# Holding retention's outgoing states, and its first incoming ones, behind gate, f and q evacuations in a hybrid decoder step

## The chip, the core and the metric

The kernel runs on one core of a Trainium2 chip. The metric is the device time of one execution in microseconds (us); the kernel before takes 2566.82 us, the median of three runs (2566.23 to 2566.89).

## The reference, cut to what matters

One decoder layer: a half-step feed-forward network, a mixer, a second half-step feed-forward network, each with a residual and a layer norm. There are 280 tokens: 16 meta tokens, 256 prompt tokens and 8 sample tokens with recurrent states of their own. All matrices are float32.

```python
q_r, k_r, v_r, g_r, q_h, f_h, i_h, g_h, a_r, a_h = jnp.split(x @ w_in, N_PROJ, axis=-1)
...
# retention, per head: the state that comes in is decayed, gets k v added, and goes out
S_new = jnp.exp(lg * C)[:, None, None].astype(S.dtype) * S + jnp.einsum('bhjd,bhjv->bhdv', k_dec, v)
...
y = jax.nn.sigmoid(a_r) * o_r + jax.nn.sigmoid(a_h) * o_h
return y @ w_out, s_ret, s_hg
```

Retention has 8 heads. For each head the 8 sample tokens bring a state of 256 x 256 numbers in and take one out: 2 MB in and 2 MB out for each head, which the kernel moves in four pieces of 512 KB. HGRN2, the other half of the mixer, has 16 heads with smaller states.

## The kernel before, in words

**Weights.** Every matrix is read once from memory in pieces of 512 KB, each with eight blocks of 128 x 128. `stream` issues such a piece as one DMA on SyncE's queue (SP) into a tile `raw` (three buffers); ScalarE (ACT) makes of it a rounded copy `whi` (L188) and VectorE (DVE) the rest `wlo` (L189); both have three buffers. For each block TensorE (PE) does three matmuls (L218): `xh,whi`, `xl,whi`, `xh,wlo`. So a piece feeds 24 matmuls. A piece can be loaded only when the piece three earlier has been split, and split only when PE is done with the piece three earlier.

**The mixer stage.** The projection `w_in` is computed in eight units, one for each retention head, counted from 0. `project` runs six groups for unit u, in the order `f`, `q_h`, `i_h`, `q_r`, `k_r`, `v_r`, and then four groups of gates of unit u-1 (`g_r` with `a_r`, `g_h` with `a_h`, twice). A group is four pieces of weights (96 matmuls), a steady unit 40 pieces. When a group is done, `evacuate` takes its sums out of PSUM: for the gates a sigmoid on ACT of each half (L690, L693, tiles `gs`) and products on DVE; for `f` a sigmoid (L653) and a scaling (L654) on ACT for each of two columns of chunks; for `q_h` a sigmoid (L660) and a product on DVE.

**Mixing in the gaps.** `mix_hg` and `mix_ret` are generators. `pump` advances them after each step of a projection, and a `yield n` lets n steps go by; so their work lies between the projection's matmuls. The order on PE is the program's. On ACT, DVE, GpSimd (POOL) and SP a scheduler sets the order from the program's, from priorities and from its own estimate of when operands are ready. A weights' DMA has high priority.

**Retention's states.** `mix_ret(u)` starts three steps after `v_r` of unit u was evacuated, that is under the gates of unit u-1. It takes tiles of one tag, `smr`, with four buffers: `ks` and `vs` (split keys and values), then two for the states' first half (`load(0)`), and when `ks` and `vs` are used up two for the second half (`load(1)`). ACT decays each piece (L1192), by a factor `gam` that POOL makes; DVE adds keys times values (L1198); then the two pieces of a half are stored to `srs` (L1202). Later PE multiplies the states with the queries (`pqr`, L1211). The buffers come free when the store has landed and `pqr` is done. In the kernel before, the states go out as soon as each half is computed, and the next unit's first half is loaded as soon as its buffers are free.

**SP's queue.** All of these loads and stores are issued by SP, one after another: a DMA whose operands aren't ready holds up all that stand behind it, weights among them.

Of the kernel before, what the change touches and what calls it, by code (L numbers as in the profile page):

```python
# [14 lines left out]
ALU = mybir.AluOpType  # L15
# [3 lines left out]
P = 128  # L19
# [9 lines left out]
HR, HG = 8, 16  # L29
# [99 lines left out]
def trunk(ctx: ExitStack, tc: tile.TileContext, A, O):  # L129
# [109 lines left out]
    def mul(out, a, b):  # L239
        nc.vector.tensor_tensor(out=out, in0=a, in1=b, op=ALU.mult)  # L240
# [306 lines left out]
    with tc.tile_pool(name="yp", bufs=1) as yp:  # L547
# [7 lines left out]
        with tc.tile_pool(name="mp", bufs=1) as mp:  # L555
# [7 lines left out]
            def tmp(name, shape=(P, T), bufs=1, dt=F32, tag=None):  # L563
                if name in rows:
                    rows[name] = rows[name][1:] + rows[name][:1]
                    return rp.tile(list(shape), dt, tag=rows[name][-1], name=name)
                return mp.tile(list(shape), dt, tag=tag or name, name=name, bufs=bufs)
# [80 lines left out]
            def evacuate(n, c0, c1, o0, o1, b0, b1):  # L648
                if n == "f":
                    f = tmp("f", (P, 2, T))  # L650
                    k = tmp("k", (P, 2, T))
                    for j, (c, o, b) in enumerate(((c0, o0, b0), (c1, o1, b1))):
                        nc.scalar.activation(f[:, j, :], o, AF.Sigmoid, **bias(b))  # L653
                        nc.scalar.activation(f[:, j, :], f[:, j, :], AF.Identity, scale=olb[:, c : c + 1], bias=lb[:, c : c + 1])  # L654
                    nc.scalar.activation(k, f, AF.Identity, scale=-1.0, bias=1.0)
                    st["f"], st["k"] = f, k
                elif n == "q_h":
                    q = tmp("q", (P, 2, TL))
                    for j, (o, b) in enumerate(((o0, b0), (o1, b1))):
                        nc.scalar.activation(q[:, j, :], o, AF.Sigmoid, **bias(b))  # L660
                        mul_biased(q[:, j, :], o, b, q[:, j, :])
                    st["q"] = q
                elif n == "i_h":
                    v = st.pop("i_h", None)
                    if v is None:
                        v = tmp("v", (P, 2, T))
                        nc.scalar.copy(v[:, 0, :], o0)
                        nc.scalar.copy(v[:, 1, :], o1)

                    start(mix_hg(c0 // 2, st["f"], st["k"], st["q"], v), {0: 20, 2: 46}.get(c0, 4))  # L670
                elif n in ("q_r", "k_r"):
                    sc, w, x0 = (1.0, TL, NMETA) if n == "q_r" else (KSC, T, 0)
                    r = tmp(n, (P, 2, w))
                    for j, (a, b, op) in enumerate(((cos, sin, ALU.subtract), (sin, cos, ALU.add))):
                        t = tmp("rot", (P, w), bufs=2)
                        for to, o, s, x in ((r[:, j, :], o0, b0, a), (t, o1, b1, b)):
                            nc.vector.scalar_tensor_tensor(
                                out=to, in0=o, scalar=sc if s is None else s, in1=x[:, x0:],
                                op0=ALU.mult if s is None else ALU.add, op1=ALU.mult)
                        nc.vector.tensor_tensor(out=r[:, j, :], in0=r[:, j, :], in1=t, op=op)  # L680
                    st[n] = r
                elif n == "v_r":
                    v = tmp("v", (P, 2, T))
                    nc.scalar.copy(v[:, 0, :], o0)
                    nc.scalar.copy(v[:, 1, :], o1)
                    start(mix_ret(c0 // 2, st["q_r"], st["k_r"], v), 24 if c0 == 2 else 3)
                elif n in ("g_r", "g_h"):
                    sg = tmp("gs", (P, TL), bufs=2)
                    t = tmp("gt", (P, TL), bufs=2)
                    nc.scalar.activation(sg, o0, AF.Sigmoid)  # L690
                    mul(t, sg, o0)
                    sa = tmp("gs", (P, TL), bufs=2)
                    nc.scalar.activation(sa, o1, AF.Sigmoid)  # L693
                    mul(t, t, sa)
                    u, e = divmod(c0, 2)
                    while u not in (done_r if n == "g_r" else done_h):
                        pump()
                    if n == "g_r":
                        y = tmp("y", (P, TL))
                        mul(y, t, on_r[u][:, e, :])  # L700
                        st["y"] = y
                    else:
                        y = st["y"]
                        nc.vector.scalar_tensor_tensor(
                            out=t, in0=t, scalar=ngt[:, c0 : c0 + 1], in1=on_h[u][:, e, :], op0=ALU.mult, op1=ALU.mult)

                        ys[c0] = y if c0 < EARLY else yp.tile([P, TL], F32, tag=f"y{c0}", name=f"y{c0}")
                        add(ys[c0], y, t)
                        if c0 < EARLY:
                            split(yh[c0], yl[c0], y)  # L710
# [374 lines left out]
            def mix_ret(u, q, k, v):  # L1085
                vt = tmp("vtr", (P, 2, 2, P))

                ks, vs = (tmp(n, (P, 2, 2, 2 * P), dt=F32R, bufs=4, tag="smr") for n in ("ks", "vs"))
                calm = 2
                sms = []  # L1090

                def load(e):
                    for c in range(2):
                        sms.append(tmp("smr", (P, 4, 256), bufs=4))
                        nc.sync.dma_start(sms[2 * e + c], A["sr"][u, c, :, 4 * e : 4 * e + 4, :])

                load(0)
# [91 lines left out]
                for e in range(2):  # L1189
                    ss = sms[2 * e : 2 * e + 2]  # L1190
                    for sm in ss:
                        nc.scalar.activation(sm, sm, AF.Copy, scale=gams[e])  # L1192
                    for i in (2 * e, 2 * e + 1):
                        for c in range(2):
                            for b in (2 * i, 2 * i + 1):
                                x, t = ss[c][:, b - 4 * e, :], LP + b
                                kk = late_k[:, c, b - 4 : b - 3] if e else k[:, c, t : t + 1]
                                nc.vector.scalar_tensor_tensor(  # L1198
                                    out=x, in0=vbs[i][:, b - 2 * i, :], scalar=kk, in1=x, op0=ALU.mult, op1=ALU.add)
                        spread(i + 2)  # L1200
                    for c in range(2):
                        nc.sync.dma_start(O["srs"][u, c, :, 4 * e : 4 * e + 4, :], ss[c])  # L1202
                    yield 1 if e else 10 if u == 0 else 6
                yield (11 if u == 0 else 15) + 2 * calm
                pq = mx_bank("pqr")
# [7 lines left out]
                                sms[2 * e + c][:, j, :], start=e + c == 0, stop=e + c == 2, tile_position=(0, 32 * j))  # L1213
                mul(scr2[:NB2], pq[:NB2, 256 : 256 + NMETA], dt[:NB2, c2:])
                upper_upper_lower(sc2, scr2[:NB2])
                os = tmp("osr", (P, 256))
                nc.scalar.copy(os, pq[:, :256])
                centre(os.unsqueeze(1))
# [158 lines left out]
```

## Time and profile before

| what | value |
|---|---|
| time, median of 3 runs | 2566.82 us (2566.23 to 2566.89) |
| span of the profiled execution, first to last instruction | 2563.9 us |
| around it, by the median of the runs | 2.9 us |
| granted TensorE clock | 1.000 |
| weights of `w_in` | 320 DMAs of 512 KB, median 4.3 us from issue to landing |
| retention's states in | 32 DMAs of 512 KB, median 5.0 us |
| retention's states out | 32 DMAs of 512 KB, median 6.7 us |

The profile is of one execution. Its span leaves out the start and the end of the program: against the median of the runs that is 2566.82 - 2563.9 = 2.9 us, and in this sense the profiled execution's own time is 2566.8 us. In rows of a timeline the first number is the start in us from the span's start, the second the duration in us. "POOL" is GpSimd, "SPq" the issue of a DMA by SyncE. In a row of a stage, the numbers behind the stretch are its length and then each engine's busy time with its count of instructions.

### The profile page before, as it was taken

To read this page: it belongs to the slowest core of one execution; us is meant where nothing else is said; L and a number is where in the kernel's file an instruction comes from. 1 tells how busy PE (TensorE), PEld (TensorE's weight loads), DVE (VectorE), ACT (ScalarE), POOL (GpSimd) and SP (SyncE) were. 2 spreads that over 40 slices of the span, in tenths; PEclk is the share of its full clock that TensorE was granted. 3 is DMA by queue.
4 is the path that set the end of the run, shared out by engine and by line. 5 is a ranking of instruction groups with operands and counts; after the bars stand their busy time and mean duration, and the time that the engine had idled before them with its cause. 6 is when DMAs were issued, how large, how long until landed. Compare 5 with 4: busy or idle time off the path is not lost.

```text
span 2563.9 us, 56275 instructions
## 1 busy us (share of the span) xinstructions
PE 2553.4 (100%) x23424; PEld 2534.4 (99%) x23424; DVE 1702.8 (66%) x2827; ACT 1392.2 (54%) x2186; POOL 57.0 (2%) x152
## 2 busy tenths in 40 slices
PE   9999999999999999999999999999999999999999
PEld 9999999999999999999999999999999999999998
DVE  6444544475569878777777777777885555556555
ACT  5444444444456767767676666675564444444443
POOL 0000000000000000000000000000000000000000
PEclk9999999999999999999999999999999999999999
DMA  7555555555555876767676767675556565565554
GB/s 244 183 187 183 187 182 184 186 182 186 184 201 180 287 265 232 264 214 260 212 264 215 259 223 255 224 239 188 196 190 197 194 197 195 194 196 195 195 195 149
DMA packets 156897, 536.26 MB, mean 209 GB/s; under 512 B 17952, under 2 KB 25952, under 8 KB 156640
## 3 DMA queue, kind: packets, MB, share of 16 engines
q1 hardware_dynamic: 156352, 532.37, 62.0%
q8 instruction: 183, 3.00, 0.5%
q14 instruction: 74, 0.61, 0.1%
q10 hardware_dynamic: 288, 0.29, 0.0%
HBM read 501.99 MB, written 30.61 MB: 208 GB/s over the span
## 4 chain that ended last, share of the span: by engine, by line
PE 96%; DVE 2%; ACT 0%; issue 0%; DMA 0%; SPq 0%; ACTq 0%; DVEq 0%
PE up L218 36%; PE dn L218 19%; PE pj_i_h L218 3%; PE pj_g_r L218 3%; PE pj_q_h L218 3%; PE pj_g_h L218 3%; PE pj_a_r L218 3%; PE pj_a_h L218 3%; PE pj_f L218 3%; PE pj_q_r L218 3%; PE pj_k_r L218 3%; PE wo L218 3%; PE pj_v_r L218 3%; DVE wlo L189 1%; PE pqr L1211 1%; PE psr L1168 0%
## 5 line engine op out<-in xcount | busy, mean ns | idle before, releaser
L189 DVE TENSOR_TENSOR wlo<-raw,whi 128x1024 fp32r<-128x1024 f32 (+1 forms) x869 | 1062.2, 1223 | 740.7 <-ACT whi L188 737.3
L188 ACT CAST whi<-raw 128x1024 fp32r<-128x1024 f32 (+1 forms) x870 | 905.7, 1042 | 909.2 <-PE up L218 411.0
L218 PE MATMUL up<-xh,whi 128*128 128x280 f32 (+1 forms) x2624 | 725.6, 280 | 0.6 <-ACT whi L188 0.6
L218 PE MATMUL up<-xh,wlo 128*128 128x280 f32 (+1 forms) x2624 | 725.8, 280 | 0.4 <-DVE wlo L189 0.3
L218 PE MATMUL up<-xl,whi 128*128 128x280 f32 (+1 forms) x2624 | 725.4, 279 | 0.0
L218 PEld LDWEIGHTS up<-xh,wlo 128*128 128x128 f32 x2624 | 492.6, 189 | 1.0 <-DVE wlo L189 1.0
L218 PEld LDWEIGHTS up<-xh,whi 128*128 128x128 f32 x2624 | 492.6, 189 | 0.8 <-ACT whi L188 0.8
L218 PEld LDWEIGHTS up<-xl,whi 128*128 128x128 f32 x2624 | 492.6, 189 | 0.0
L218 PE MATMUL dn<-hh,whi 128*128 128x280 f32 (+1 forms) x1376 | 384.7, 280 | 0.0
L218 PE MATMUL dn<-hh,wlo 128*128 128x280 f32 (+1 forms) x1376 | 384.3, 279 | 0.0
L218 PE MATMUL dn<-hl,whi 128*128 128x280 f32 (+1 forms) x1376 | 384.3, 279 | 0.0
L218 PEld LDWEIGHTS dn<-hh,whi 128*128 128x128 f32 x1376 | 260.1, 189 | 0.1
L218 PEld LDWEIGHTS dn<-hl,whi 128*128 128x128 f32 x1376 | 260.1, 189 | 0.1
L218 PEld LDWEIGHTS dn<-hh,wlo 128*128 128x128 f32 x1376 | 260.1, 189 | 0.0
L218 PE MATMUL pj_k_r<-xh,whi 128*128 128x280 f32 x256 | 74.2, 290 | 0.0
L218 PE MATMUL pj_g_r<-xh,whi 128*128 128x264 f32 x256 | 74.0, 289 | 0.0
L218 PE MATMUL pj_v_r<-xh,whi 128*128 128x280 f32 x256 | 73.8, 288 | 0.0
L218 PE MATMUL pj_v_r<-xh,wlo 128*128 128x280 f32 x256 | 72.4, 283 | 0.3 <-DVE wlo L189 0.3
L218 PE MATMUL pj_g_h<-xh,whi 128*128 128x264 f32 x256 | 72.7, 284 | 0.0
L218 PE MATMUL pj_k_r<-xh,wlo 128*128 128x280 f32 x256 | 72.4, 283 | 0.0
L218 PE MATMUL pj_v_r<-xl,whi 128*128 128x280 f32 x256 | 72.3, 283 | 0.0
L218 PE MATMUL pj_k_r<-xl,whi 128*128 128x280 f32 x256 | 72.3, 283 | 0.0
(421 smaller groups left out, 5263.4 us busy)
## 6 DMA issues: line engine op xcount, KB each, us to landing
raw<-in_w_up SPq DMA_DIRECT2D x343, 512.0 KB, 4.1
raw<-in_w_in SPq DMA_DIRECT2D x320, 512.0 KB, 4.3
raw<-in_w_dn SPq DMA_DIRECT2D x172, 512.0 KB, 3.5
smr<-in_sr SPq DMA_DIRECT2D x32, 512.0 KB, 5.0
out_srs<-smr SPq DMA_DIRECT2D x32, 512.0 KB, 6.7
raw<-in_w_out SPq DMA_DIRECT2D x32, 512.0 KB, 3.9
vbr<-vrd SPq DMA_DIRECT2D x32, 256.0 KB, 4.1
smh<-in_sg SPq DMA_DIRECT2D x16, 512.0 KB, 5.2
```

The lines of the kernel that those rows point to most:

```text
L188: nc.scalar.copy(hi[:, j:jn, :], raw[:, j:jn, :])
L189: nc.vector.tensor_tensor(out=lo[:, j0:j1, :], in0=raw[:, j0:j1, :], in1=hi[:, j0:j1, :].bitcast(F32), op=ALU.subtract)
L218: nc.tensor.matmul(o, w, t, start=start, stop=stop)
L1211: nc.tensor.matmul(pq[32 * j : 32 * j + 32, :256], qdr_at[c][:, 32 * b : 32 * b + 32], sms[2 * e + c][:, j, :], start=e + c == 0, stop=e + ...
```

## The change

It has three parts, all for units u > 1, that is for six of the eight:

- The stores of a unit's states aren't issued when the states are ready. A new generator, `outgoing`, is started where `pqr` is multiplied, 23 steps later it handles the first half and another 16 steps later the second. For each half POOL copies one column into a tile `zero`, clears it, and adds it to one column of each of the half's two pieces; then the pieces are stored. The column copied is the last gate's sigmoid (`st["seen"]`) for the first half and the next unit's `f` for the second (in the last unit, which has no next, the latest gate's sigmoid again). So a store waits, by way of POOL, for that evacuation. What is added is zero; the states stay the same.
- Before each of the two DMAs of `load(0)`, POOL copies one column of `st["q"]`, the HGRN2 queries of the unit itself, into the buffer, which makes the load wait for the evacuation of `q_h`.
- `evacuate` notes the gate's sigmoid in `st["seen"]`.

```diff
                     nc.scalar.activation(sa, o1, AF.Sigmoid)
+                    st["seen"] = sa
...
                 calm = 2
+                held = u > 1
                 sms = []
 
                 def load(e):
                     for c in range(2):
                         sms.append(tmp("smr", (P, 4, 256), bufs=4))
+                        if e == 0 and u > 1:
+                            nc.gpsimd.tensor_copy(sms[c][:, 0, :1], st["q"][:, 0, :1])
                         nc.sync.dma_start(sms[2 * e + c], A["sr"][u, c, :, 4 * e : 4 * e + 4, :])
...
-                    for c in range(2):
-                        nc.sync.dma_start(O["srs"][u, c, :, 4 * e : 4 * e + 4, :], ss[c])
+                    if not held:
+                        for c in range(2):
+                            nc.sync.dma_start(O["srs"][u, c, :, 4 * e : 4 * e + 4, :], ss[c])
...
                 upper_upper_lower(sc2, scr2[:NB2])
+                if held:
+
+                    def outgoing():
+                        for e in range(2):
+                            zero = tmp("zero", (P, 1))
+                            nc.gpsimd.tensor_copy(zero, st["f"][:, 0, :1] if e and u < HR - 1 else st["seen"][:, :1])
+                            nc.gpsimd.memset(zero, 0.0)
+                            for c in range(2):
+                                sm = sms[2 * e + c]
+                                nc.gpsimd.tensor_tensor(out=sm[:, 0, :1], in0=sm[:, 0, :1], in1=zero, op=ALU.add)
+                                nc.sync.dma_start(O["srs"][u, c, :, 4 * e : 4 * e + 4, :], sm)
+                            yield 16
+
+                    start(outgoing(), 23)
```

The built programs show what the scheduler makes of it. On PE, ACT and DVE the order of all instructions is as before, apart from line numbers. POOL gets 60 instructions more, ten for each of the six units, and SP's queue is ordered anew. The places below are of unit 5, and the pieces of `w_in` bear their numbers: `raw218` is the 219th of 320.

First SP's queue in the kernel before, under the gates of unit 4. `out_srs` is the states' way out, `in_sr` their way in; the two `in_sr` are the next unit's first half.

```order
L185 DMA raw218_18933<-in_w_in 128x1024
L1202 DMA out_srs<-smr_18505 128x1024
L185 DMA raw219_19011<-in_w_in 128x1024
L1202 DMA out_srs<-smr_18507 128x1024
L185 DMA raw220_19052<-in_w_in 128x1024
L185 DMA raw221_19121<-in_w_in 128x1024
L1202 DMA out_srs<-smr_18707 128x1024
L185 DMA raw222_19151<-in_w_in 128x1024
L1202 DMA out_srs<-smr_18709 128x1024
L185 DMA raw223_19206<-in_w_in 128x1024
L1095 DMA smr_20334<-in_sr 128x1024
L1095 DMA smr_20336<-in_sr 128x1024
```

With the change nothing but weights stands there (and `dtab` behind `raw225`, as before). The stores now stand ten pieces further on, behind `raw228`, where SP issues the weights of `q_h` of unit 6:

```order
L185 DMA raw228_19443<-in_w_in 128x1024
L1231 DMA out_srs<-smr_18541 128x1024
L185 DMA raw229_19480<-in_w_in 128x1024
L1231 DMA out_srs<-smr_18544 128x1024
L185 DMA raw230_19510<-in_w_in 128x1024
L185 DMA raw231_19540<-in_w_in 128x1024
L185 DMA raw232_19577<-in_w_in 128x1024
L1231 DMA out_srs<-smr_18745 128x1024
L185 DMA raw233_19607<-in_w_in 128x1024
L185 DMA raw234_19637<-in_w_in 128x1024
L1231 DMA out_srs<-smr_18747 128x1024
L185 DMA raw235_19667<-in_w_in 128x1024
```

The next unit's loads follow a little later on the same queue:

```order
L185 DMA raw236_19702<-in_w_in 128x1024
L1099 DMA smr_20382<-in_sr 128x1024
L185 DMA raw237_19756<-in_w_in 128x1024
L1099 DMA smr_20385<-in_sr 128x1024
L185 DMA raw238_19834<-in_w_in 128x1024
```

So six transfers of 512 KB move from between `raw218` and `raw224` to between `raw228` and `raw238`, and each of `raw229`, `raw230`, `raw233`, `raw235`, `raw237` and `raw238` stands right behind one that waits for POOL. The loads of unit 2 move alone (from around `raw70` to behind `raw77` and `raw78`), since the stores of unit 1 stay where they are, and the stores of unit 7 move alone, since no unit follows.

POOL's queue in the kernel before, from the last instruction of retention's unit 5 on (`sro` holds the late keys, `meta` and `ends` belong to HGRN2 of unit 6):

```order
L1188 COPY sro_18722<-k_r_18280 128x8
L910 COPY meta_8644<-K_19688 128x2x16
L750 COPY ends_19684<-v_19649 128x2x16
L751 COPY ends_19684<-v_19649 128x2x16
```

And with the change (the tiles `smr` are the states; `gs` is the gate's sigmoid, `q` the HGRN2 queries of unit 6):

```order
L1192 COPY sro_18760<-k_r_18316 128x8
L1226 COPY zero_19313<-gs_19287 128x1
L1227 MEMSET zero_19313 128x1
L1230 TENSOR_TENSOR smr_18541<-smr_18541,zero_19313 128x1
L1230 TENSOR_TENSOR smr_18544<-smr_18544,zero_19313 128x1
L1226 COPY zero_19461<-f_19434 128x1
L1227 MEMSET zero_19461 128x1
L1230 TENSOR_TENSOR smr_18745<-smr_18745,zero_19461 128x1
L1230 TENSOR_TENSOR smr_18747<-smr_18747,zero_19461 128x1
L911 COPY meta_8644<-K_19736 128x2x16
L1098 COPY smr_20382<-q_19570 128x1
L1098 COPY smr_20385<-q_19570 128x1
```

The eight new instructions of the stores stand ahead of `meta`, the two of the loads ahead of `ends`.

## The prediction

> **What bounds the kernel now.** I read the page first, then the busy times of the mixer's units, the chain of waits, the DMAs of two short windows, and last the timelines of ACT, DVE, POOL and SP in one unit.
>
> ```profile
> span 2563.9 us, 56275 instructions
> ...
> PE 2553.4 (100%) x23424; PEld 2534.4 (99%) x23424; DVE 1702.8 (66%) x2827; ACT 1392.2 (54%) x2186; POOL 57.0 (2%) x152
> ```
>
> PE is busy but for 10.5 us of the whole span. A busy PE may still be slowed, so the stage with the change is looked at by itself. The rows below are stretches of one unit each; the change acts in all of them, from the loads of unit 2 in the first to the stores of unit 7, which reach past the last.
>
> ```profile
> core 0: us, PE busy (x) PEld busy (x) DVE busy (x) ACT busy (x) POOL busy (x), PEclk, DMA share, GB/s
> 963.80:1090.16 126.36, 126.36 (x1299) 124.16 (x1298) 104.12 (x223) 94.49 (x188) 6.42 (x14) 1.00 0.72 245
> 1090.16:1216.50 126.34, 126.34 (x1276) 124.67 (x1276) 98.49 (x195) 84.80 (x158) 6.16 (x14) 1.00 0.70 239
> 1216.50:1342.83 126.33, 126.33 (x1276) 124.67 (x1276) 98.49 (x195) 84.70 (x157) 6.18 (x14) 1.00 0.71 239
> 1342.83:1469.16 126.33, 126.33 (x1276) 124.66 (x1276) 98.75 (x195) 84.51 (x158) 6.16 (x14) 1.00 0.71 239
> 1469.16:1595.50 126.34, 126.34 (x1277) 124.67 (x1276) 98.49 (x195) 84.73 (x158) 6.46 (x14) 1.00 0.71 239
> 1595.50:1721.90 126.40, 126.40 (x1278) 124.73 (x1278) 98.48 (x195) 84.64 (x159) 7.19 (x25) 1.00 0.69 229
> ```
>
> In each, PE's busy time is the stretch itself, at a granted clock of 1.00, and the units agree to 0.07 us. Nothing that varies, as a wait for a transfer would, is in them. Next the pace, from the chain of waits (start, us, matmuls):
>
> ```profile
> 10.35 488.37 PE up L218 x4096
> ...
> 1476.31 10.80 PE pj_q_h L218 x96
> 1487.11 11.44 PE pj_i_h L218 x96
> ...
> 1527.80 6.44 PE pj_v_r L218 x54
> ```
>
> A matmul of 280 columns takes 488.37 / 4096 = 119.2 ns in the first feed-forward network, where the queue carries nothing but weights, and 11.44 / 96 = 119.2 ns in the mixer, so the mixer's matmuls aren't slowed by what else is moved. `q_h`, with 264 columns, takes 10.80 / 96 = 112.5 ns. PE's order is the same after the change. What bounds units 2 to 7 is PE at full pace: nothing there can be gained by moving a transfer, and all that can be lost is a weight that comes late.
>
> **What is removed.** The six transfers leave the stretch under the gates. The two windows below are the DMAs before: first 24 us with the burst of unit 5 (1432 to 1456), then 43 us behind it (1457 to 1500), where they go. A queue's row has packets, MB and the share of 16 engines; the others the median us from issue to landing.
>
> ```profile
> q1 hardware_dynamic: 2292, 7.77, 94.0%
> ...
> raw<-in_w_in SPq DMA_DIRECT2D x8, 512.0 KB, 6.4
> out_srs<-smr SPq DMA_DIRECT2D x4, 512.0 KB, 6.7
> smr<-in_sr SPq DMA_DIRECT2D x2, 512.0 KB, 8.0
> ```
>
> ```profile
> q1 hardware_dynamic: 2136, 7.67, 53.9%
> ...
> raw<-in_w_in SPq DMA_DIRECT2D x15, 512.0 KB, 3.9
> ```
>
> In the burst the DMA engines are full and weights need 6.4 us; behind it 3.9 us. Taking six transfers of 0.52 MB out leaves 7.77 - 3.15 = 4.62 MB, 56% by the same measure, and weights there should land in about 4 us. Gain on PE: 0, since PE doesn't wait there. One 512 KB transfer occupies the engines for 24 x 0.94 x 0.524 / 7.77 = 1.5 us.
>
> **What is added to the calm stretch.** It gets 3.15 MB to 7.67 MB, so 53.9% becomes about 76%: under the 94% of the burst. The transfers are covered as a mean; what remains is single pieces of weights that stand on SP's queue right behind a store or load that waits for POOL. The rows of unit 5, where unit 6 is projected, ACT and DVE:
>
> ```profile
> 1467.49 0.39 ACT L693 ACTIVATE gs<-pj_a_h 128x264 f32<-128x264 f32 x1
> ...
> 1474.48 1.03 ACT L188 CAST whi<-raw 128x1024 fp32r<-128x1024 f32 x1
> ...
> 1478.06 0.62 ACT L654 ACTIVATE f<-f,lb,olb 128x280 f32<-128x280 f32 x1
> ...
> 1484.34 1.05 ACT L188 CAST whi<-raw 128x1024 fp32r<-128x1024 f32 x1 [0.69 <-PE pj_q_h L218]
> ```
>
> ```profile
> 1475.89 1.22 DVE L189 TENSOR_TENSOR wlo<-raw,whi 128x1024 fp32r<-128x1024 f32 x1
> ...
> 1485.42 1.23 DVE L189 TENSOR_TENSOR wlo<-raw,whi 128x1024 fp32r<-128x1024 f32 x1
> ...
> 1487.79 0.42 DVE L240 TENSOR_TENSOR q<-q,pj_q_h 128x264 f32<-128x264 f32 x1
> ```
>
> The casts at 1474.48 and 1484.34 are those of raw229 and raw233. SP's issues of raw229, raw233 and raw237, each from its timeline:
>
> ```profile
> 1468.51 0.33 SPq L185 DMA_DIRECT2D raw<-in_w_in  x1
> ```
>
> ```profile
> 1479.45 0.33 SPq L185 DMA_DIRECT2D raw<-in_w_in  x1
> ```
>
> ```profile
> 1489.93 0.33 SPq L185 DMA_DIRECT2D raw<-in_w_in  x1
> ```
>
> The trace has no POOL addition of two tiles. Its bounds are the cheapest and the dearest POOL instruction of one column, and a clear:
>
> ```profile
> 1514.40 0.19 POOL L773 COPY vbh<-acch 128x1 f32<-128x1 f32 x1 [12.67 <-DVE acch L836]
> ```
>
> ```profile
> 1549.18 1.17 POOL L1174 TENSOR_SCALAR gam<-sro 128x1 f32<-128x1 f32 x1 [9.91 <-ACT sro L1170]
> 1551.58 0.10 POOL L1186 MEMSET sro<- 128x1 f32 x1 [1.22 <-issue]
> ```
>
> ```profile
> 1549.10 1.21 DVE L189 TENSOR_TENSOR wlo<-raw,whi 128x1024 fp32r<-128x1024 f32 x1
> ```
>
> So copy, clear and add take 0.19 + 0.10 + 0.19 = 0.48 us at the least, 1.17 + 0.10 + 1.17 = 2.44 us at the most. The dear one lies under a `wlo` and ends with it (1549.18 + 1.17 = 1550.35, 1549.10 + 1.21 = 1550.31). The Trainium skill, page "SBUF — State Buffer", section "Who interferes with whom", has GpSimd and VectorE share a pair of ports as a lock held for a whole instruction, and the loser blocks: the row agrees, and by the page a new addition could in turn hold up a `wlo`. By the page alone, with every new copy and addition behind a `wlo`, the chain is at its dear end, and the loss worked out below is still 0. A cheap one that comes first would cost DVE 0.19 us; DVE is busy 98.5 us of 126.3. I take a chain in the middle, 1.5 us, as DVE is that busy.
>
> **Three places.** An issue by SP I take at 0.45 us, a little over a weight's 0.33.
>
> *raw229, behind the first store.* The gate's sigmoid ends at 1467.88; with POOL's chain the store can be issued at 1468.4 to 1470.3, and raw229 at 1468.8 to 1470.8 where it was 1468.51. With 3.9 us and 1.5 us for the store ahead it lands at 1474.2 to 1476.2. Its cast began at 1474.48: it is late by 0 to 1.7 us. The cover: `wlo` ended at 1477.11, and PE comes to raw229 after raw228's 24 matmuls, at 1476.31 + 24 x 0.1125 = 1479.01. That is 1.9 us. Loss 0, with 0.2 us to spare at the dear end.
>
> *raw233, behind the third store.* The first column of `f` ends at 1478.68; store at 1479.2 to 1481.1, raw233 at 1479.6 to 1481.6 instead of 1479.45, landing 1485.0 to 1487.0 against a cast at 1484.34: late by 0.7 to 2.7 us. `wlo` ended at 1486.65; PE needs it at 1487.11 + 24 x 0.1192 = 1489.97. Cover 3.3 us. Loss 0. Between the two places the cast before was released by PE (the row at 1484.34), so lateness of the first place doesn't carry over.
>
> *raw237, behind the first load.* The queries' column ends at 1488.21, one POOL copy later, at 1488.4 to 1489.4, the load is issued, and SP is free before 1489.93. Loss 0.
>
> **What else hangs on it.** Behind the eight new instructions POOL has `meta`, behind the two copies `ends`:
>
> ```profile
> 1485.14 0.22 POOL L910 COPY meta<-K 128x32 f32<-128x32 f32 x1 [59.75 <-DVE T L240]
> 1500.61 0.97 POOL L750 COPY ends<-v 128x32 f32<-128x32 f32 x1 [15.25 <-ACT v L668]
> ```
>
> Both waited for DVE and ACT long after the new ones are through: cost 0. POOL itself, at 2%, gets 60 x 0.19 to 60 x 1.17, or 11 to 70 us over six units. The held buffers are wanted again by the next unit's `ks` and `vs`, after `v_r`, which is still being multiplied at 1527.80; the last store, issued by about 1482.5, has landed by 1490. The loads land by about 1499 at the burst's 8.0 us; their decay follows `gam` at 1549.18. In unit 7 the stores wait for gates, and no loads follow.
>
> **Sum:** 2563.9 + 0 in the span, 2.9 us around it: 2566.8 us.
>
> **The rivals.**
>
> *Weights late (slower).* The wait stands on the issuing engine, and all weights behind it stand too. The Trainium skill, page "DMA: Bandwidth & Descriptors", section "Anatomy of one DMA", says that DMA engines don't wait on semaphores but the sequencer does before it issues; that is the rule that speaks against this change. It decides from a landing of raw229 after 1474.48 + 1.9 = 1476.4. With the dear chain, issue at 1470.8, and the burst's 6.4 us it lands at 1477.2, 0.8 us over; with the slowest row, 8.0 us, at 1478.8, 2.4 us over. In the five units 2 to 6, where `f` and `q_h` follow, that is 4 to 12 us, middle 8: 2574.8 us. For it: three transfers within a microsecond at raw229, and a thin cover. Against it: nothing else is on the queue there.
>
> *The burst costs PE something now (faster).* If transfers slowed matmuls, the mixer's pace would differ from 119.2 ns; it doesn't. The most there could be is all of PE's idle time, 10.5 us, with half of it 2561.6 us; no row of these units shows any.
>
> *The change doesn't do what it says.* Were each wait met before SP comes to it, the moved queue order alone would spread the transfers: 2566.8 us too, and only the profile tells it apart.
>
> **How the numbers follow.** No change 0.92 (the third rival, 0.3 of it, gives the same time), weights late 0.06, faster 0.02. A measurement of this kernel can tell about 0.2%, 5.1 us, from no change; the first rival's lower half lies under that, and its 0.06 is for what exceeds it. The range: below, the fastest run of before less the three runs' spread, 2566.23 - 0.66 = 2565.6; above, 0.3 us of late weights in each of six units, 2566.8 + 1.8 = 2568.6.
>
> **What would show it.** Right: the units' stretches again at 126.3 us with PE busy throughout; in the window of the former burst weights landing in about 4 us at 56%; in the calm one about 76%; POOL's additions between 0.19 and 1.17 us; raw229 issued up to 2.3 us later, its cast late by under 1.9 us. Wrong: PE idle before `q_h`'s second piece or `i_h`'s second, released by `whi` or `wlo`, and units of over 127 us.

## The result, and the profile after

The changed kernel takes 2579.43 us (median of 4 runs, 2577.91 to 2579.79) against 2566.53 us (median of 4 runs) for the kernel before: a ratio of 1.0048, interval 1.0036 to 1.0060. It is slower by 12.9 us, and the interval lies clear of 1. The profiled execution took 2579.79 us, with a span 14.1 us longer than that of before. In the executions with both on record the time is 1.7 to 1.9 us above the span, so the profiled execution of before took some 2565.7 us (an estimate), 0.8 us less than the median; that, with the 0.4 us above the median after, makes 14.1 of 12.9. One execution of those below, with the loads alone, took 6932.23 us at a granted clock of 1.00; it isn't explained, and the ratios leave it out. The forecast of no change was wrong.

The head of the page after:

```profile
span 2578.0 us, 56363 instructions
...
PE 2558.2 (99%) x23424; PEld 2536.3 (98%) x23424; DVE 1701.3 (66%) x2827; ACT 1391.9 (54%) x2186; POOL 75.0 (3%) x212
```

PE stands idle for 19.8 us instead of 10.5, and is busy for 4.8 us more with as many matmuls; 9.3 + 4.8 is the 14.1 us. DVE and ACT are no busier, and POOL's 18 us would fit its idle time many times over. The stretches of the six units, cut at the same instructions as those of before (length, then PE busy):

```profile
core 0: us, PE busy (x) PEld busy (x) DVE busy (x) ACT busy (x) POOL busy (x), PEclk, DMA share, GB/s
964.10:1091.70 127.60, 126.65 (x1300) 124.28 (x1299) 103.85 (x222) 94.58 (x188) 7.68 (x20) 1.00 0.66 221
1091.70:1220.53 128.83, 126.97 (x1277) 124.67 (x1276) 98.36 (x195) 84.69 (x158) 8.56 (x24) 1.00 0.70 234
1220.53:1349.27 128.74, 127.01 (x1276) 124.72 (x1276) 98.47 (x195) 84.70 (x159) 8.56 (x24) 1.00 0.69 234
1349.27:1476.89 127.62, 126.75 (x1276) 124.61 (x1275) 98.40 (x195) 84.48 (x157) 8.57 (x24) 1.00 0.72 237
1476.89:1604.38 127.49, 126.74 (x1276) 124.66 (x1276) 98.47 (x195) 84.50 (x159) 8.56 (x24) 1.00 0.70 237
1604.38:1734.84 130.46, 128.49 (x1279) 126.39 (x1279) 98.35 (x195) 84.57 (x158) 10.56 (x35) 0.99 0.67 230
```

Against 126.3 to 126.4 us before, the units of these stretches (2 to 7) lose 1.2, 2.5, 2.4, 1.3, 1.2 and 4.1 us, 12.6 us together; most of the rest is 1.15 us at unit 7's stores. Unit 2, whose stretch moves two loads and no store, loses too. What PE waited for, over the whole span (total, times, longest):

```profile
PE pt L879 <- POOL ends L752: 5.8, 6, 1.8
PE pt L876 <- ACT v L667: 1.9, 2, 1.0
...
PE pj_g_r L218 <- DVE wlo L189: 0.8, 1, 0.8
```

All three rows are new. No wait for a weight of `q_h` or `i_h` is among them; the third is a weight of the gates that comes late behind unit 7's stores. The first two stand where no step of the prediction looked: at the transposes `pt` at the start of HGRN2 (`mix_hg`), which take `v`, the evacuation of `i_h` by ACT, and `ends`, two small copies of `v` by POOL. In unit 6, after and then before, PE's last of these transposes:

```profile
1511.04 0.30 PE L879 MATMUL pt<-ident,ends 128*64 128x128 f32 x1 [0.75 <-POOL ends L752]
```

```profile
1502.20 0.27 PE L878 MATMUL pt<-ident,ends 128*64 128x128 f32 x1
```

The second copy of `ends` before:

```profile
1501.53 0.20 POOL L751 COPY ends<-v 128x32 f32<-128x32 f32 x1
```

It was through at 1501.73, and PE came at 1502.20: 0.47 us to spare. The same difference is 0.2 to 0.5 us in units 3, 4, 5 and 7, and 0.06 us in unit 2, where the second copy takes 1.21 us. Now to what made it late. ACT in unit 6 after (in brackets its idle time and what ended it):

```profile
1490.76 0.62 ACT L907 COPY kept<-K 128x512 f32<-128x512 f32 x1 [0.20 <-DVE K L240]
1493.67 1.04 ACT L188 CAST whi<-raw 128x1024 fp32r<-128x1024 f32 x1 [2.29 <-DMA raw<-in_w_in]
...
1496.34 0.40 ACT L919 COPY kept<-K 128x256 f32<-128x256 f32 x1 [1.32 <-DVE K L240]
...
1507.87 0.40 ACT L922 COPY Qm<-Q 128x256 f32<-128x256 f32 x1 [1.32 <-DVE Q L240]
1508.18 0.39 ACT L667 COPY v<-pj_i_h 128x280 f32<-128x280 f32 x1
...
1509.41 0.40 ACT L668 COPY v<-pj_i_h 128x280 f32<-128x280 f32 x1
```

and the same instructions before:

```profile
1487.01 0.41 ACT L918 COPY kept<-K 128x256 f32<-128x256 f32 x1 [1.32 <-DVE K L240]
...
1498.62 0.41 ACT L921 COPY Qm<-Q 128x256 f32<-128x256 f32 x1 [1.32 <-DVE Q L240]
1498.93 0.39 ACT L667 COPY v<-pj_i_h 128x280 f32<-128x280 f32 x1
...
1500.16 0.39 ACT L668 COPY v<-pj_i_h 128x280 f32<-128x280 f32 x1
```

Up to `kept` at 1490.76 everything in this unit stands 7.73 us later than before (1483.03), which is what the units ahead have lost. The next instruction is the cast of raw233. It waited 0.69 us for PE before, and waits 2.29 us for its transfer now: 1.60 us later. From there to `v`, 15 us on, ACT and DVE carry that delay almost undiminished: 1496.34 - 1487.01 = 9.33, and 1508.18 - 1498.93 = 9.25. The idle times of 1.32 us on the way are the same in both kernels: ACT waits there for a product of DVE that itself stands behind a `wlo`, which waits for ACT's cast. One gap ahead of a cast, 1.00 us at 1489.93 before, does close, and the cast behind it is only 0.49 us late (1498.15); but the copy behind that cast waits for DVE and is 1.60 us late again (1500.33 against 1491.00). The two queues hand work to each other in a fixed order, and their gaps give back 0.08 of the 1.60 us.

What raw233 waited for, in SP's queue:

```profile
1484.89 0.33 SPq L185 DMA_DIRECT2D raw<-in_w_in  x1
1487.67 0.34 SPq L1231 DMA_DIRECT2D out_srs<-smr  x1
1488.10 1.54 SPq L185 DMA_DIRECT2D raw<-in_w_in  x2
```

SP stands at the third store until POOL's chain is through, so raw233 is issued at 1488.10, 0.92 us late (1479.45 + 7.73 = 1487.18), and the store's 512 KB stand ahead of it. The DMAs in the window of the former burst, 1439.5 to 1463, and in the calm one, 1464.7 to 1508:

```profile
q1 hardware_dynamic: 1488, 4.86, 65.0%
...
raw<-in_w_in SPq DMA_DIRECT2D x8, 512.0 KB, 4.1
```

```profile
q1 hardware_dynamic: 2875, 10.47, 69.6%
...
raw<-in_w_in SPq DMA_DIRECT2D x15, 512.0 KB, 5.1
out_srs<-smr SPq DMA_DIRECT2D x4, 512.0 KB, 4.5
```

Weights land in 4.1 us instead of 6.4 where nobody waits for them, and in 5.1 us instead of 3.9 where ACT does. POOL in unit 6, and the last copies of `ends` in unit 7:

```profile
1486.56 0.65 POOL L1226 COPY zero<-f 128x1 f32<-128x1 f32 x1 [9.74 <-ACT f L654]
1487.27 0.10 POOL L1227 MEMSET zero<- 128x1 f32 x1
1487.45 0.34 POOL L1230 TENSOR_TENSOR smr<-smr,zero 128x1 f32<-128x1 f32 x2
...
1509.86 0.98 POOL L751 COPY ends<-v 128x32 f32<-128x32 f32 x1 [11.96 <-ACT v L668]
1510.78 0.21 POOL L752 COPY ends<-v 128x32 f32<-128x32 f32 x1
```

```profile
1638.42 1.30 POOL L752 COPY ends<-v 128x32 f32<-128x32 f32 x1
```

In unit 7 the second copy takes 1.30 us instead of 0.21: it began with a `wlo` of DVE (1638.41 to 1639.64) and ended with it. That is the one stall of 1.84 us.

The other units go the same way. Set against the first matmul of `q_h` in its unit, the cast of the piece in raw233's place is 1.6 to 2.0 us late in units 3 to 7, the second copy of `ends` ends 1.15, 2.83, 2.76, 1.46, 1.53 and 2.80 us late in units 2 to 7, and PE comes out of the transposes 1.15, 2.47, 2.33, 1.31, 1.11 and 2.36 us late: 10.7 of the 13 us. In units 3 and 4 the cast of the piece behind the first load waits for its transfer too, and adds 1.1 and 0.8 us on the same queue; in unit 2 that is the only delay.

### The profile page after: what moved, and what is told of

Read it like the earlier page. It is cut to its first block, busy times and chain, and to the rows that moved or that the text cites. A ratio compares the mean times of both kernels' runs of the same rounds, so it can differ in the third digit from the quotient of the medians.

```text
span 2578.0 us, 56363 instructions
## 1 busy us (share of the span) xinstructions
PE 2558.2 (99%) x23424; PEld 2536.3 (98%) x23424; DVE 1701.3 (66%) x2827; ACT 1391.9 (54%) x2186; POOL 75.0 (3%) x212
## 4 chain that ended last, share of the span: by engine, by line
PE 88%; DVE 5%; issue 3%; ACT 2%; DMA 2%; POOL 0%; SPq 0%; ACTq 0%; POOLq 0%; DVEq 0%
PE up L218 36%; PE dn L218 19%; PE pj_g_r L218 3%; PE pj_a_r L218 3%; PE pj_k_r L218 3%; PE wo L218 3%; PE pj_v_r L218 3%; PE pj_g_h L218 3%; PE pj_a_h L218 3%; PE pj_q_r L218 2%; PE pj_f L218 2%; DVE wlo L189 2%; PE pj_q_h L218 2%; DMA raw<-in_w_in 1%; ACT whi L188 1%
```

## The experiments

The theory, "late cast": a transfer of 512 KB ahead of raw233 (and, in units 2 to 4, the first load ahead of the next piece) makes a cast late; nobody misses the weights, but the cast stands in ACT's queue ahead of `v`, and PE has at most 0.5 us to spare at `ends`. The rivals: "POOL" (the new instructions hold up DVE, or `ends` behind them) and "traffic" (3.15 MB more in the calm stretch, wherever they stand). All expectations were written ahead of their runs, those of later groups with the earlier ones known. Each time stands beside the kernel before on the same chip.

**POOL alone.** The sixty instructions stay in place but work on tiles of their own; the DMAs are those of before.

```diff
-                            nc.gpsimd.tensor_copy(sms[c][:, 0, :1], st["q"][:, 0, :1])
+                            nc.gpsimd.tensor_copy(pad[:, c : c + 1], st["q"][:, 0, :1])
...
-                                nc.gpsimd.tensor_tensor(out=sm[:, 0, :1], in0=sm[:, 0, :1], in1=zero, op=ALU.add)
-                                nc.sync.dma_start(O["srs"][u, c, :, 4 * e : 4 * e + 4, :], sm)
+                                nc.gpsimd.tensor_tensor(out=pad[:, c : c + 1], in0=pad[:, c : c + 1], in1=zero, op=ALU.add)
```

> POOL's sixty new instructions stand where the change puts them, but work on a tile of their own; the six transfers stay in the order and at the places of the kernel before. Theory 'late cast' (the third store and the loads delay raw233 and raw237, the late cast stands in ACT's queue ahead of i_h's evacuation v, and PE waits for v and ends): no loss, 2566.5 us, within 1 us of the kernel before. Rival 'POOL' (the new instructions block VectorE, or stand ahead of ends): the whole loss, 2577 to 2580 us.

2567.32 us against 2566.93 (ratio 1.0001, 0.9992 to 1.0010). POOL's instructions cost nothing that can be told from no change; that rival falls. The trace has one stall for `ends` all the same, 0.4 us in unit 7: the piece in raw233's place was cast 1.10 us late there, though it was issued within 0.03 us of its old place and no transfer was moved. PE lost 0.6 us there. So a late landing also comes by chance.

**The loads alone.** The stores go out as before.

```diff
-                held = u > 1
+                held = False
```

> The stores go out as before; only the next unit's two first loads wait for the queries. 'Late cast': unit 2, where the change moves nothing but loads, loses its 1.4 us again; in units 3 to 7 the store that made raw233 late is gone and raw237's lateness alone is 0 to 0.8 us each, so 2568 to 2572 us, 2569.5 the likeliest, with raw233 cast as early as before. Rival 'traffic' (1.05 MB of the 3.15 MB more in the calm stretch): a third of the loss, 2570 to 2571 us, so this run alone does not part them. Rival 'POOL': two of the ten instructions of a unit, but the two that stand just ahead of ends: most of the loss, 2575 us or more.

2568.18 us against 2566.93 (1.0004, 0.9995 to 1.0013). The total can't be told from no change; the trace has two stalls for `ends`, in units 2 and 3 (at 998 and 1126 us):

```profile
PE pt L879 <- POOL ends L752: 1.6, 2, 0.9
```

The first is the loads'. In unit 2 raw78 stands right behind the first load; it was issued on time, but its cast waited for the transfer and was 1.25 us late, with 0.06 us to spare at `ends`:

```profile
995.68 1.05 ACT L188 CAST whi<-raw 128x1024 fp32r<-128x1024 f32 x1 [1.23 <-DMA raw<-in_w_in]
```

The second is not: raw113, in raw233's place in unit 3, was issued on time at 1102.10, before that unit's loads, and took 5.99 us to land; that is a late landing by chance, as in the run before. In units 4 to 7 the loads, moved alone, cost nothing.

**The first half's stores alone.**

```diff
-                    if not held:
+                    if e or not held:
...
-                        for e in range(2):
+                        for e in range(1):
```

with the loads as before.

> Only the two stores of the first half wait for the gate; the second half's stores and all loads stay as before. 'Late cast': raw229 was cast on time in the changed kernel, so nothing in units 3 to 7; at most 1.2 us at unit 7's stores: 2566.5 to 2567.7 us. Rival 'traffic': a third of the loss, 2570 to 2571 us. Rival 'POOL': four of the ten instructions of a unit, 2569 us or more.

2567.01 us against 2566.93 (1.0000, 0.9991 to 1.0009), with no new wait at `pt`. By the medians, loads and first half, each moved alone, account for 1.25 + 0.08 = 1.3 of 13 us.

**All four stores behind the gate.** The second half no longer waits for `f`; SP meets the third store with its wait long met.

```diff
-                            nc.gpsimd.tensor_copy(zero, st["f"][:, 0, :1] if e and u < HR - 1 else st["seen"][:, :1])
+                            nc.gpsimd.tensor_copy(zero, st["seen"][:, :1])
```

> The whole change, but the second half's stores wait for the gate's sigmoid too, not for the next f: the same bytes in the calm stretch, and SP meets the third store when POOL is long through. 'Late cast': raw233 is issued on time and nothing is ahead of it on the DMA engines for long; what remains is unit 2's 1.4 us, 0 to 0.8 us of the loads in five units and 1.2 us at unit 7's stores: 2569 to 2573 us. Rival 'traffic': as the changed kernel, 2577 to 2580 us. Rival 'POOL': two instructions of a kind moved by 10 us, still ahead of ends: 2577 to 2580 us.

2575.48 us against 2566.93 (1.0036, 1.0024 to 1.0048): less than the whole change's loss, but more than I expected. In this order the third store stands ahead of raw232 and the fourth ahead of raw233, and four stores go out within 9 us; from 1474 to 1500 us weights land in 5.5 us (median). The casts of raw232 and raw233 in unit 6 wait for their transfers, though SP issued both within 0.03 us of their old places:

```profile
1489.93 1.05 ACT L188 CAST whi<-raw 128x1024 fp32r<-128x1024 f32 x1 [0.87 <-DMA raw<-in_w_in]
...
1492.88 1.05 ACT L188 CAST whi<-raw 128x1024 fp32r<-128x1024 f32 x1 [1.39 <-DMA raw<-in_w_in]
```

They are 0.97 and 1.38 us late. So a transfer just ahead does harm without a wait.

**`ends` by DVE.** The whole change, but the two copies move from POOL to DVE.

```diff
-                nc.gpsimd.tensor_copy(ends[:, :, 0, :], v[:, :, :NMETA])
-                nc.gpsimd.tensor_copy(ends[:, :, 1, :], v[:, :, T - NMETA :])
+                nc.vector.tensor_copy(ends[:, :, 0, :], v[:, :, :NMETA])
+                nc.vector.tensor_copy(ends[:, :, 1, :], v[:, :, T - NMETA :])
```

> The whole change, but VectorE copies v's two ends instead of POOL. 'Late cast': the delay of v stays, but the 0.7 to 0.9 us that PE stood for ends after v goes in six units, and with it the one copy of 1.30 us with the 1.84 us stall and the slower matmuls behind it; v's own waits of 1.0 and 0.9 us and unit 7's stores stay: 2570 to 2574 us. If ends only carries the wait's name and v's lateness is all, nothing changes: 2578 to 2580 us.

2578.59 us against 2567.32 (1.0043, 1.0031 to 1.0056). The long stall of unit 7 is gone, but not the others: DVE's copies take 0.17 us each, and stand behind a `wlo`, in the same late queue:

```profile
1509.13 1.23 DVE L189 TENSOR_TENSOR wlo<-raw,whi 128x1024 fp32r<-128x1024 f32 x1 [0.81 <-ACT whi L188]
1510.28 0.17 DVE L751 COPY ends<-v 128x32 f32<-128x32 f32 x1
```

My expectation of 2570 to 2574 us missed that. A shorter copy on a queue that is late as well gains nothing.

**The slack at `ends`.** The kernel before, with POOL made to come late.

```diff
+                if u > 1:
+                    for _ in range(8):
+                        nc.gpsimd.tensor_copy(ends[:, 1, 0, :1], v[:, 1, T - 1 :])
```

> The kernel before, with eight copies of one column by POOL ahead of the second half of ends in units 2 to 7: no DMA is moved, only ends comes later. It prices the slack. 'Late cast' holds that PE had about 0.5 us to spare at ends and stands one for one behind that: with ends 1.5 to 2 us later, PE idle 1.0 to 1.6 us in each of six units, 2572 to 2577 us, and 2583 to 2587 us if each stall is followed by 16 slow matmuls as the one of 1.84 us was. If the PE wait on ends is not what costs the time: 2566.5 us.

2589.94 us against 2567.32 (1.0085, 1.0071 to 1.0099): more than I expected, since one of the copies fell under a `wlo`, which made the stalls 2.3 to 3.5 us long, and four of the six were followed by slow matmuls (last section). POOL in unit 6:

```profile
1521.01 2.67 POOL L752 COPY ends<-v 128x1 f32<-128x1 f32 x7
1523.74 0.21 POOL L753 COPY ends<-v 128x32 f32<-128x32 f32 x1
```

`ends` is through at 1523.95. This unit's offset to the kernel before is 19.4 us, so that is 2.8 us late, and PE stood 2.27 us in the profile's count and lost 2.4 us: some 0.4 us of slack, and one for one behind it.

**The second half and the loads.** The first half's stores go out as before.

```diff
-                    if not held:
+                    if not (held and e):
...
-                        for e in range(2):
+                        for e in (1,):
...
-                    start(outgoing(), 23)
+                    start(outgoing(), 39)
```

> Only the second half's stores (behind f) and the next unit's loads are moved; the first half's stores go out as before. 'Late cast': raw233 is as late as in the changed kernel, so units 3 to 7 lose 8.5 to 11.5 us, unit 2 its 1.4 us, unit 7's stores up to 1.2 us: 2576 to 2580 us. If the loss comes of six transfers together (traffic), with four of six and none near raw229: 2570 to 2574 us.

2579.13 us against 2567.32 (1.0045, 1.0032 to 1.0057): 11.8 us, by the interval the whole loss, with four of six transfers moved. One stall of 1.26 us in the trace, at 943 us and ahead of every moved transfer, is not the change's: the run with a late `ends`, which moves none, has one of 0.96 us there. The cast of raw233 in unit 6 waits 2.17 us for its transfer, as in the changed kernel.

**The same stores two pieces later.** The whole change, with the second half waiting for `k` in place of `f`.

```diff
-                            nc.gpsimd.tensor_copy(zero, st["f"][:, 0, :1] if e and u < HR - 1 else st["seen"][:, :1])
+                            nc.gpsimd.tensor_copy(zero, st["k"][:, 0, :1] if e and u < HR - 1 else st["seen"][:, :1])
```

> The whole change, but the second half's stores wait for k (2.5 us after f's first column), so they stand ahead of raw235 and raw236 and not of raw233 and raw235; as many bytes, waits and POOL instructions. 'Late cast': raw233 is in time again; raw235 had 1.46 us between landing and cast, raw236 2.0 us, about what a transfer ahead costs, so units 4 to 7 lose 0 to 0.5 us each; unit 2 1.4, unit 3 0.8, unit 7's stores 1.2: 2569.5 to 2573 us. Rival 'traffic': 2577 to 2580 us.

2569.57 us against 2567.32 (1.0010, 1.0001 to 1.0019): as many bytes and waits, and ten of the 13 us gone. The cast of raw233 in unit 6 is released by PE as before, and the unit's stretch, 1472.28 to 1598.60, has its old length of 126.32 us, with PE busy throughout:

```profile
1487.46 1.05 ACT L188 CAST whi<-raw 128x1024 fp32r<-128x1024 f32 x1 [0.68 <-PE pj_q_h L218]
```

The DMAs of its calm stretch, 1460.1 to 1503.4:

```profile
q1 hardware_dynamic: 2913, 10.62, 68.8%
```

"Traffic" falls: the changed kernel has 10.47 MB and 69.6% there. Weights land in 4.2 us here (median) against 5.1. It is not how much, but ahead of which piece.

**ACT late, nothing moved.** The kernel before, with the first sigmoid of `q_h`'s evacuation taken six times. (DVE's first product of `q` goes one `wlo` later with it.)

```diff
-                        nc.scalar.activation(q[:, j, :], o, AF.Sigmoid, **bias(b))
+                        for _ in range(6 if c0 > 2 and j == 0 else 1):
+                            nc.scalar.activation(q[:, j, :], o, AF.Sigmoid, **bias(b))
```

> The kernel before, with no transfer and no POOL instruction moved; ScalarE takes the first sigmoid of q_h's evacuation five times more in each of units 2 to 7, about 0.3 us each, so that its queue is some 1.5 us late from q on, as the late cast of raw233 made it. 'Late cast' (the delay runs down ScalarE's and VectorE's queues to v and ends, while the weights themselves stay in time): PE loses the 1.5 us less 0.4 to 0.5 us of slack in each of six units, 2572 to 2575 us, waiting at v or ends. If what hurts is only weights or transfers that come late: no loss, 2566 to 2568 us.

2571.34 us against 2567.05 (1.0016, 1.0007 to 1.0025), a little less than expected, because part of the extra time went into idle time ahead of the next cast. In unit 6 `v` stands at 1503.55 where 1498.93 + 3.71 = 1502.64 would be on time, 0.91 us late, and PE lost 0.48 us there. All of its new waits are of the kind of the changed kernel:

```profile
PE pt L879 <- POOL ends L752: 2.7, 6, 1.1
```

A late queue on ACT and DVE is enough, with every transfer where it was.

**The wait alone.** All stores and loads go out as in the kernel before. In units 2 to 6 SP also waits for `f` and POOL as in the change, ahead of raw233 and raw235, but what it then sends is one column. (The lines are set against those of the change.)

```diff
-                                nc.gpsimd.tensor_tensor(out=sm[:, 0, :1], in0=sm[:, 0, :1], in1=zero, op=ALU.add)
-                                nc.sync.dma_start(O["srs"][u, c, :, 4 * e : 4 * e + 4, :], sm)
+                                scr = drp.tile([P, 1], F32, tag="held", name="held")
+                                nc.gpsimd.tensor_tensor(out=zero, in0=zero, in1=zero, op=ALU.add)
+                                nc.sync.dma_start(scr, zero)
```

> All stores and loads as before; in units 2 to 6 POOL still copies f's first column, clears and adds, and SP still waits for it ahead of raw233 and raw235, but what it then sends is one column (512 B) to a tile of its own. The wait alone delays raw233's issue by 0.9 us against 0.98 us between its landing and its cast before. If the transfer ahead of raw233 is what makes its cast late, no loss: 2566 to 2568.5 us. If SP's wait for POOL is: the second half's share, 2573 to 2577 us.

2610.91 us against 2567.05 (1.0171, 1.0158 to 1.0185), far outside both. The run measured something else. The DMAs issued from 1506.5 to 1516.2:

```profile
raw<-in_w_in SPq DMA_DIRECT2D x2, 512.0 KB, 11.6
held<-zero SPq DMA_DIRECT2D x2, 0.5 KB, 9.1
```

A store of one column of 128 partitions, 512 bytes, took 9.1 us to land, longer than 512 KB in one piece (4.5 us in the changed kernel), and the weights behind it took 11.6 us; the second POOL addition waited for the first store as well. It tells nothing of the wait. The next run sends one row in place of the column:

```diff
-                                scr = drp.tile([P, 1], F32, tag="held", name="held")
+                            scr = drp.tile([1, 16], F32, tag="held", name="held")
```

> The wait alone again, with a store that is small in packets too: all stores and loads as before; in units 2 to 6 POOL copies 16 elements of f's first row, clears and adds, and SP waits for it ahead of raw233 and sends 64 bytes of one row to a tile of its own (and the same once more ahead of raw234, with POOL through). If the transfer of 512 KB ahead of raw233 is what makes its cast late, no loss, since 0.9 to 1.5 us of wait meet 0.98 us between landing and cast and 0.4 us of slack at v: 2566 to 2568.5 us. If SP's wait for POOL is: the second half's share, 2573 to 2577 us.

2567.64 us against 2566.85 (1.0003, 0.9994 to 1.0013). The cast of raw233 in unit 6 waits for its transfer, 1.09 us instead of 0.69:

```profile
1485.78 1.04 ACT L188 CAST whi<-raw 128x1024 fp32r<-128x1024 f32 x1 [1.09 <-DMA raw<-in_w_in]
```

It is 0.40 us late, which the slack just covers, though SP issued raw233 0.84 us late (1481.33 against 1479.45 and this unit's offset of 1.04), almost as late as in the changed kernel. In units 3, 4 and 5 the cast in that place is at most 0.31 us late. In unit 7 it is 1.11 us late and PE lost 0.6 us, but the run with POOL alone was 1.10 us late there with SP on time, so that can't be put down to the wait. Of the 1.60 us in unit 6 of the changed kernel SP's wait is thus the smaller part, and the transfer ahead the larger; the shares rest on this one unit.

**The transposes later.** The whole change with all its queues, but PE comes to `pt` 18 matmuls later.

```diff
-                    start(mix_hg(c0 // 2, st["f"], st["k"], st["q"], v), {0: 20, 2: 46}.get(c0, 4))
+                    start(mix_hg(c0 // 2, st["f"], st["k"], st["q"], v), {0: 20, 2: 46}.get(c0, 7))
...
                 if steady:
-                    yield 6
+                    yield 3
```

> The whole change, with nothing taken off the queues, but PE meets the transposes of v and ends 18 matmuls (2.0 us) later in each unit from 2 on, and the step behind them waits as much less. 'Late cast': v and ends, 1 to 2.3 us too late, are then in time, and no weight was late for PE; what remains is unit 7's stores, 0.8 us, and a few tenths: 2567 to 2570 us. If PE loses its time to weights, to transfers or to POOL's instructions themselves: 2576 to 2580 us, as the changed kernel.

2570.60 us against 2566.85 (1.0014, 1.0005 to 1.0023). In unit 6 the cast of raw233 is as late as ever, and PE goes through the transposes without a stop:

```profile
1490.15 1.04 ACT L188 CAST whi<-raw 128x1024 fp32r<-128x1024 f32 x1 [2.48 <-DMA raw<-in_w_in]
```

```profile
1508.25 0.27 PE L879 MATMUL pt<-ident,ends 128*64 128x128 f32 x1
```

What is left of the loss, 3.75 us, is for the most part a new wait of 1.8 us for `K` in unit 2, one of 0.8 us at unit 7's stores and one of 0.6 us for `ends`. No version tried beats the kernel before, as PE has no idle time in these units to win back.

## Why the prediction was wrong

The step that failed is "What else hangs on it", with its "cost 0", and under it the way that "Three places" took a loss: a late weight was priced by when PE needs the weight, and by nothing else.

- *What bounds the kernel.* PE at full pace, nothing to gain: right. "All that can be lost is a weight that comes late" was too narrow: PE also waits for evacuations, through transposes that stand in its own order.
- *What is removed.* Gain 0, weights in about 4 us: right (4.1 us; the share was 65% where 56% was forecast). The calm stretch came to 69.6%, below the 76%. As a mean this was fine, and the mean decided nothing.
- *POOL's chain.* 0.65 + 0.10 + 0.19 us and the gaps, about 1 us, inside the bounds of 0.48 and 2.44; one addition of 24, in unit 7, took 1.24 us, above the bound of 1.17. The first run shows no cost of the instructions. The Trainium skill, page "SBUF — State Buffer", section "Who interferes with whom", has VectorE and GpSimd hold a shared pair of ports for a whole instruction; the trace agrees at the copy of 1.30 us under a `wlo`, and where that cost PE time, in unit 7, it was an existing copy that was held up, not a new one.
- *raw229.* Late by 0 to 1.7 us, loss 0: right. Its cast was on time (1482.23, 7.75 us after its old place, in a unit that started 7.73 us late), and the first half alone cost nothing.
- *raw233.* Late by 0.7 to 2.7 us, cover 3.3 us at PE: both right. The cast was 1.60 us late, and PE never waited for the weight. The loss of 0 was wrong: the same cast stands in ACT's queue ahead of fourteen more instructions and then `v`, whose reader had 0.4 to 0.5 us to spare. The prediction looked at what stands behind the new instructions on SP and POOL, and not at what stands behind the late cast on ACT and DVE.
- *raw237.* On time by the prediction, which charged 1.5 us for the store ahead at raw229 and raw233, and nothing here for the load ahead. In unit 6 that did no harm. In unit 2 it was the whole loss (raw78, 1.2 us late, PE 1.15 us), and in units 3 and 4 it added 1.1 and 0.8 us to a queue that was late already.
- *`ends`.* The quoted row, 15.25 us of idle time ended by ACT's `v`, was read as ample room. It says that `ends` starts when `v` is through: the room to look for was behind it, 0.47 us up to PE's transpose.
- *Unit 7.* "The stores wait for gates" was given no price. They cost 1.15 us, of which 0.8 us is a wait for a `wlo` of `pj_g_r`: the weight that comes late for PE, which the prediction had looked for in units 2 to 6 alone.
- *The rivals.* "Weights late" had the sign and 8 of 13 us, by way of raw229 and a wait at PE that was not seen in units 2 to 6; agreement in size is chance. The chance of 0.06 was far too small, as each cover had been checked against one reader alone.
- *The sum.* Its 2.9 us around the span were 1.8 us and a profiled execution some 1.1 us faster than the median of three; that moved nothing in the forecast of no change.

What the stalls cost beyond their length is in part a slower PE. The first 2 us behind the stall of unit 6 and behind that of unit 7, in the changed kernel:

```profile
1511.10:1513.10 2.00, 2.00 (x19) 2.00 (x20) 1.24 (x2) 1.35 (x6) 0.00 (x0) 1.00 0.48 158
1639.80:1641.80 2.00, 2.00 (x10) 2.00 (x11) 0.28 (x1) 1.33 (x6) 0.00 (x0) 0.55 0.61 231
```

Behind 1.84 us of idle time PE took ten matmuls in 2 us where it takes 19. From 1639.82 to 1643.35 it started 16 in 3.5 us, where they take 16 x 0.1125 = 1.8 us: 1.7 us more. Unit 7's 4.1 us are 2.0 us idle and 2.1 us of busier PE; the 0.4 us that remain, and the 0.3 to 0.7 us by which PE is busier in the other units, were not traced.

## What to carry to other kernels

A piece of input that comes late is charged to every instruction behind its first reader, not only to the engine that needs it in the end: follow the reader's own queue (here ACT, and DVE in turn with it) to the next point where the busiest engine meets its output, and take the slack there. Idle time on a helper engine that alternates with another is no slack if each gap is ended by the other. When moving transfers into a calm stretch, look for the pieces with the least time between landing and use and keep 512 KB from standing right ahead of them; moving two stores by two pieces gave back ten of 13 us with the same bytes.

## What the runs showed of the hardware

PE's pace after a stall. Stalls of up to 1.77 us (the new wait in the run with the later transposes) were not followed by slow matmuls. Both of 1.84 us were, in the changed kernel and in the run with the second half, and so were all five of 2.3 to 3.6 us in the run that stored one column, two of them only behind a second stall of 0.75 us, 1.3 us on. In the run with a late `ends`, the one of 3.5 us and three of the five of 2.3 to 2.5 us were, and two were not; the 2 us behind that of 3.5 us, and behind one of those two:

```profile
1002.60:1004.60 2.00, 2.00 (x10) 2.00 (x11) 0.56 (x2) 1.50 (x6) 0.00 (x0) 0.50 0.01 2
1264.60:1266.60 2.00, 2.00 (x19) 2.00 (x20) 0.28 (x1) 1.39 (x6) 0.00 (x0) 1.00 0.01 2
```

The slow stretches have 13 to 24 matmuls of 0.22 to 0.23 us, 3 to 5.6 us. The Trainium skill, page "TensorE: Matmul & The Clock Gate", "Part 1: The HAM clock gate", has the clock halve after an idle window of about 3.4 us and come back after as much work, with windows that run free of the kernel. The length of the slow stretches and the chance in it agree; the idle time does not, as 1.84 us were enough.

A store's cost by its shape: 512 bytes as one column of 128 partitions took 9.1 us from issue to landing, and the weights behind it 11.6 us; 512 KB in one piece took 4.5 us.
